# Input projection of a hybrid decoder layer: convolution passes alternate with value, gate and output gate passes

## The chip, the cores and the metric

The kernel runs on one core of one Trainium2 chip. The metric is the device time of one launch in microseconds. Five engines work side by side, each through its own queue in order: TensorE (PE, matmuls and transposes), VectorE (DVE), ScalarE (ACT), GpSimd (POOL) and SyncE (SP, which issues most of the DMAs). An instruction waits for its inputs by semaphores, and everything behind it on its engine waits with it. On-chip tiles come from pools: a name (or a tag) has a number of buffers (`bufs`), and a new tile of that name waits until the oldest one is no longer used.

## The reference

One inference step of a layer with two kinds of heads that share one input projection `z = x @ w_in` (1024 to 3600 columns) over 2048 prompt tokens and 64 sampled tokens:

```python
fq, fk, fv = z[..., 0:512], z[..., 512:1024], z[..., 1024:1536]      # attention heads
flogf = log_sigmoid(z[..., 1536:1544] + b_fox_f)
qk_in = z[..., 1544:2568]                                             # memory heads
xpad = concatenate([conv_prev, qk_in], axis=1)
conv = conv_b + xpad[:, 0:S] * conv_w[0]
for j in range(1, CONV_WIDTH):
    conv = conv + xpad[:, j:j + S] * conv_w[j]
qk = silu(conv)
mv = z[..., 2568:3080]
ig, lf = z[..., 3080:3084] + b_ig, log_sigmoid(z[..., 3084:3088] + b_fg)
og = sigmoid(z[..., 3088:] + b_og)
```

Then come attention with forget gates over the prompt (`_fox_prompt`) and, for the sampled tokens, over 8192 cached positions in pages (`_fox_sample`); the matrix memory in chunks (`_mlstm_chunk`: gates, `Wqk @ v + q @ C`, normaliser, new `C` and `n`); the output projection with a layer norm; and an MLP with squared ReLU and a second layer norm. Keys, values, gates, memory states and the last three convolution inputs are outputs too.

## The kernel before

The kernel has four phases: A, the input projection; B, the prompt's attention (`phase_b`); O, the output projection (`phase_o`); C, the MLP (`phase_c`). The change lies in phase A, which takes up to 991 us.

**Blocks and passes.** `block_a(bi)` (L395) handles one of four blocks of 512 prompt tokens; block 0 has the 64 sampled tokens too (`pre`, tile 16). The block's input stands transposed in `xT[bi]`, split into a high and a low part. A pass takes 256 columns of `w_in`: `wload` (L212) loads them in two halves, ACT makes the high part (`whi`, L130), DVE the low one (`wlo`, L133), and `mm3` (L137) does three matmuls for each product (L138 to L140). Passes are of two layouts. In `natural` (L399) tokens are the output's partitions, and a `sink` takes each token tile out of PSUM; in the convolution and query loops columns are the partitions, with groups of 256 tokens (320 with the sampled ones). All results go through four PSUM buffers of one tag, `pm`. A block has 14 passes in this order:

- two value passes, v0 and v1 (L417 to L424); ACT copies the tiles out, SP stores them to `dv`; v1 carries 16 gate columns too, which DVE copies to `gat`;
- in block 0, `conv_setup` (L180) loads and transposes the convolution weights and old convolution inputs;
- four convolution passes, c0 to c3, of two column tiles `j` each (L429 to L464). ACT copies the sums to `qi` (L447); DVE does one multiplication with bias (L453), three multiply-adds over 128x512 (L455) and, after ACT's tanh (L457), the product (L458); SP stores `th` to `dqk` (L459). `ac` and `th` share the tag `ac` with three buffers. In block 0 there is a second, short convolution for the sampled tokens with each `j`, and then the new convolution state goes to `scT` (L464);
- the transposes of the convolution state for the outputs (L466 to L482), in blocks 0 and 3;
- `yield 1` (L483), by which `block_a` hands control back once;
- two output gate passes, og0 and og1 (L484 to L493): DVE adds the bias (L489), ACT does tanh (L490), DVE scales (L491), SP stores to `dog`; then `gated.add(bi)`;
- two query passes, two key passes and two value passes of the attention heads (L496 to L534); ACT takes the sums out, SP stores them.

**What runs beside the passes.** After each PSUM group a pass calls `tick(us)` (L109) with its nominal time: 2.6 for a token tile, 2.56 or 3.2 for a column group. Two streams of small work are generators that `tick` advances by a step. The memory stream `macc` makes a step per `PACE_M` = 2.3 us of ticks and holds a list: `gate_stream` (gates and their cumulated sums, put at the head of the list after v1, L427), then `m_block` of the block (L597), in block 0 preceded by the `prologue` of the sampled attention, and after block 0 `m_sample` (L677), which loads `state_C` into `C0` (L739) for each of four heads. `m_block` has 4 steps and then 7 for each chunk of 128 tokens: exponentials of the loaded `Wm` and `qa`, scores (L622), `while bi not in gated: yield 1` (L628), the load of the gates `og`, transposed keys (L635), outputs (L647, L648), normalising (`h_out`, `norm_out`, with POOL's product at L557), the new state (L656, L659); the transposes of the outputs (L562) are left to the next chunk (`turn_out`). The sampled attention `acc` makes a step per 7.5 us of ticks from the end of block 0 on: POOL gathers pages of keys (`kraw`, L1359), DVE transposes them (L1361), TensorE multiplies (L1372), and after eight pairs of pages there is a softmax (L1383: scores L1390, exponentials L1406, transposes L1416, L1433) and products with the values (L1451).

**What sets the order.** The program is recorded in this order, and a scheduler then places each engine's instructions by its own estimate of when their inputs are ready; `beside` (L102) keeps a stream's step behind the latest matmul, ACT split and DVE split of the pass. On the chip the order is fixed. The loop that drives it is at L807: `next(g)` runs a block up to its `yield 1`, then `m_block(bi)` is appended to the list, and `for _ in g` runs the rest.

```python
    for bi in range(4):
        g = block_a(bi)
        next(g)
        if bi == 0 and gen:
            macc[1].append(prologue(gen))
        macc[1].append(m_block(bi))
        for _ in g:
            pass
```

Of the kernel before, what the change touches and what calls it, by code (L numbers as in the profile page):

```python
# [23 lines left out]
PACE_M = 2.3  # L24
# [28 lines left out]
def body(ctx, tc, I, O, stages):  # L53
# [43 lines left out]

    acc = [0.0, None, PACE_A]
    macc = [0.0, []]
    last = {}  # L100

    def beside(gen):  # L102
# [6 lines left out]
    def tick(us):  # L109

        macc[0] += us
        while macc[1] and macc[0] > PACE_M:
            macc[0] -= PACE_M
            if beside(macc[1][0]) == 0:
                macc[1].pop(0)
        if not macc[1]:
            macc[0] = 0.0
        acc[0] += us
        while acc[1] is not None and acc[0] > acc[2]:
            acc[0] -= acc[2]  # L120
            if beside(acc[1]) == 0:
                acc[1] = None
# [14 lines left out]
    def mm3(ps, wh, wl, xh, xl, first, stop):  # L137
        T.matmul(ps, wh, xh, start=first, stop=False)  # L138
        T.matmul(ps, wh, xl, start=False, stop=False)  # L139
        last["PE"] = T.matmul(ps, wl, xh, start=False, stop=stop)  # L140
# [254 lines left out]
    def block_a(bi):  # L395
# [18 lines left out]
            A.copy(st, ps)  # L414
            return st

        for i in range(2):  # L417
            def sink(t, m, ps, i=i):
                r = tok_r(t)
                SY.dma_start(dv[r:r + m, i * 256:(i + 1) * 256], stage(ps[:, :256], m, 256))  # L420
                if i == 1:
                    V.tensor_copy((gats if t == 16 else gat[:, t])[:, 0:16], ps[:, 256:272])
            natural(sink, (C_V + i * 256, 256), *([(C_FF, 8), (C_I, 8)] if i == 1 else []),
                    hook=None if i else lambda n: load_x(bi, blk[n + 2:n + 3]))  # L424
        if bi == 0:
            conv_setup()
        macc[1].insert(0, gate_stream(bi))  # L427

        for j in range(8):  # L429
            if j % 2 == 0:  # L430
                wh, wl = wload([(C_QK + j * 128, 256)])
            cs = slice((j % 2) * 128, (j % 2) * 128 + 128)
            qi = pa.tile([128, 515], F32, name="qi", bufs=2)
            V.tensor_copy(qi[:, 0:3], hist[:, j])
            if pre:
                qs = pa.tile([128, 8, 11], F32, name="qs", bufs=2)
                V.tensor_copy(qs[:, :, 0:3], scT[:, j])
            for i in range(2):
                xh, xl = xT[bi][i]
                w = 256 + (pre if i == 0 else 0)  # L440
                ps = ppa.tile([128, 512], F32, name="pm", tag="pm", bufs=4)[:, :w]
                for k in range(8):
                    mm3(ps, wh[k][:, cs], wl[k][:, cs], xh[:, k, :w], xl[:, k, :w], k == 0, k == 7)
                tick(w * 0.01)
                if w == 320:
                    A.copy(qs[:, :, 3:11], ps[:, 0:64].rearrange("p (b t) -> p b t", t=8))
                A.copy(qi[:, 3 + i * 256:259 + i * 256], ps[:, w - 256:])  # L447
            V.tensor_copy(hist[:, j], qi[:, 512:515])

            def conv(src, dst, n):  # L450
                ac = pa.tile([128, 512], F32, name="ac", tag="ac", bufs=3)[:, :n]
                acv = ac if len(src(0).shape) == 2 else ac.rearrange("p (b t) -> p b t", t=8)
                V.tensor_scalar(acv, src(0), cw[:, j, 0:1], cw[:, j, 4:5], op0=OP.mult, op1=OP.add)  # L453
                for q in range(1, 4):
                    V.scalar_tensor_tensor(acv, src(q), cw[:, j, q:q + 1], acv, op0=OP.mult, op1=OP.add)  # L455
                th = pa.tile([128, 512], F32, name="th", tag="ac", bufs=3)[:, :n]
                A.activation(th, ac, AF.Tanh)  # L457
                V.scalar_tensor_tensor(th, th, 1.0, ac, op0=OP.add, op1=OP.mult)  # L458
                SY.dma_start(dst, th)  # L459

            conv(lambda q: qi[:, q:q + 512], dqk[j, :, t0:t0 + 512], 512)
            if pre:
                conv(lambda q: qs[:, :, q:q + 8], dqk[j, :, S:], 64)
                V.tensor_copy(scT[:, j], qs[:, :, 8:11])  # L464

        if pre:  # L466

            cs_n = pa.tile([24, 1024], F32, name="cs_n", tag="xn", bufs=2)
            for hf in range(2):
                pc = ppa.tile([24, 512], F32, name="px", tag="pm", bufs=4)  # L470
                for j in range(4):
                    T.transpose(pc[:, j * 128:(j + 1) * 128], scT[:, hf * 4 + j].rearrange("p b k -> p (b k)"), ident)
                A.copy(cs_n[:, hf * 512:(hf + 1) * 512], pc)
            SY.dma_start(O["conv_sample"].rearrange("l b j c -> (l b j) c"), cs_n)
        if bi == 3:
            ch_n = pa.tile([3, 1024], F32, name="ch_n", tag="xn", bufs=2)
            for hf in range(2):
                pc = ppa.tile([3, 512], F32, name="px", tag="pm", bufs=4)
                for j in range(4):
                    T.transpose(pc[:, j * 128:(j + 1) * 128], hist[:, hf * 4 + j], ident)  # L480
                A.copy(ch_n[:, hf * 512:(hf + 1) * 512], pc)
            SY.dma_start(O["conv_prompt"].rearrange("l b j c -> (l b j) c"), ch_n)  # L482
        yield 1  # L483
        for i in range(2):  # L484
            def sink(t, m, ps, i=i):
                r = tok_r(t)
                cs = slice(i * 256, (i + 1) * 256)
                st = pa.tile([128, 256], F32, name="st", bufs=4)[:m]
                V.tensor_tensor(st, ps, bog[:m, cs], op=OP.add)  # L489
                A.activation(st, st, AF.Tanh, scale=0.5)  # L490
                V.scalar_tensor_tensor(st, st, 1.0, nwh[:m, cs], op0=OP.add, op1=OP.mult)  # L491
                SY.dma_start(dog[r:r + m, cs], st)
            natural(sink, (C_O + i * 256, 256))  # L493
        gated.add(bi)

        for j in range(4):  # L496
            if j % 2 == 0:
                wh, wl = wload([(j * 128, 256)])
                if pre:
                    qr = ps_.tile([32, 8, 8, 8], F32, name="qr", bufs=1)  # L500
            cs = slice((j % 2) * 128, (j % 2) * 128 + 128)
            st = pa.tile([128, 512], F32, name="qst", tag="ac", bufs=3)
            for i in range(2):
                xh, xl = xT[bi][i]
                w = 256 + (pre if i == 0 else 0)
                ps = ppa.tile([128, 512], F32, name="pm", tag="pm", bufs=4)[:, :w]
                for k in range(8):
                    mm3(ps, wh[k][:, cs], wl[k][:, cs], xh[:, k, :w], xl[:, k, :w], k == 0, k == 7)
                tick(w * 0.01)
                if w == 320:  # L510
                    for c in range(4):
                        V.tensor_scalar(qr[:, :, (j % 2) * 4 + c], ps[c * 32:c * 32 + 32, 0:64].rearrange("p (b t) -> p b t", t=8), 0.125, None, op0=OP.mult)
                A.activation(st[:, i * 256:i * 256 + 256], ps[:, w - 256:], AF.Copy, scale=0.125)
            SY.dma_start(dq[j, :, t0:t0 + 512], st)
            if pre and j % 2 == 1:
                SY.dma_start(dqb[0, :, :, j // 2 * 64:j // 2 * 64 + 64].rearrange("b p c -> p b c"), qr.rearrange("p b i t -> p b (i t)"))
        for i in range(2):
            def sink(t, m, ps, i=i):
                d = k_out(t)[:, i * 256:(i + 1) * 256]
                if t == 16:  # L520
                    if i == 0:
                        sqk.append(ps_.tile([64, 512], F32, name="sqk", tag="vt", bufs=2))
                    st = sqk[0][:, i * 256:(i + 1) * 256]
                    A.copy(st, ps)
                else:
                    st = stage(ps, m, 256)
                SY.dma_start(d, st)
            natural(sink, (512 + i * 256, 256))
        for i in range(2):
            def sink(t, m, ps, i=i):  # L530
                d = v_out(t)[:, i * 256:(i + 1) * 256]
                SY.dma_start(d, stage(ps, m, 256))
            natural(sink, (1024 + i * 256, 256),
                    hook=None if i == 0 or bi == 3 else lambda n: load_x(bi + 1, BLKS[bi + 1][0:1]) if n == len(blk) - 1 else None)  # L534

    dgs_s = drm.tile([4, 8], F32, name="dgs_s")

# [267 lines left out]
    first = [wload([(C_V, 256)])]  # L805
    load_x(0, [0])
    for bi in range(4):  # L807
        g = block_a(bi)
        next(g)
        if bi == 0 and gen:  # L810
# [701 lines left out]
```

## Time and profile before

| | |
|---|---|
| median of 3 runs | 3477.34 us (3472.2 to 3483.77) |
| profiled execution | 3490.14 us, its span 3488.4 us |
| mean granted TensorE clock | 0.98 |
| phase A | from 13.4 us (first projection matmul) to 991.2 us (last one) |
| HBM traffic | 598.01 MB read, 61.22 MB written, 189 GB/s over the span |

In the profile an engine is busy while it executes an instruction; waiting, branching and issuing of DMAs do not count. A window's row gives the length, the busy time of PE, PEld (weight loads, which overlap PE), DVE, ACT and POOL with the number of instructions, the clock granted to TensorE (1.00 is full), the busy share of the DMA engines and GB/s. A row of waits has the engine and the line that waited, what released it, the sum in us, how often, and the longest. A row of the chain or of the timeline has the start, the duration and the work. `pm<-whi,xh` is a tile and what it is made from.

### The profile page before, as it was taken

To read this page: it belongs to the slowest core of one execution; us is meant where nothing else is said; L and a number is where in the kernel's file an instruction comes from. 1 tells how busy PE (TensorE), PEld (TensorE's weight loads), DVE (VectorE), ACT (ScalarE), POOL (GpSimd) and SP (SyncE) were. 2 spreads that over 40 slices of the span, in tenths; PEclk is the share of its full clock that TensorE was granted. 3 is DMA by queue.
4 is the path that set the end of the run, shared out by engine and by line. 5 is a ranking of instruction groups with operands and counts; after the bars stand their busy time and mean duration, and the time that the engine had idled before them with its cause. 6 is when DMAs were issued, how large, how long until landed. Compare 5 with 4: busy or idle time off the path is not lost.

```text
span 3488.4 us, 59559 instructions
## 1 busy us (share of the span) xinstructions
PE 3347.1 (96%) x22428; PEld 2674.8 (77%) x22428; DVE 2176.1 (62%) x5282; ACT 1369.4 (39%) x2818; POOL 903.2 (26%) x962
## 2 busy tenths in 40 slices
PE   8899899999989999999899999999999999999998
PEld 8898788888876666667567677776677777788887
DVE  5847756657568787655556567656666544654555
ACT  3332233334358888512323233332233333343332
POOL 0023222321332222266332324313334111100000
PEclk9999899999999999999899999999999999999999
DMA  5567786775853232586776767858768555442221
GB/s 175 167 172 231 224 248 222 240 227 189 277 165 86 76 81 58 169 289 228 264 237 200 266 215 263 281 181 281 241 218 300 183 174 174 140 154 73 85 85 64
DMA packets 446040, 663.15 MB, mean 190 GB/s; under 512 B 84604, under 2 KB 333760, under 8 KB 444856
## 3 DMA queue, kind: packets, MB, share of 16 engines
q1 hardware_dynamic: 369064, 380.13, 36.2%
q0 software_dynamic: 74304, 270.57, 22.3%
q10 hardware_dynamic: 2384, 8.65, 0.7%
q8 instruction: 176, 2.88, 0.3%
q14 instruction: 112, 0.92, 0.1%
HBM read 598.01 MB, written 61.22 MB: 189 GB/s over the span
## 4 chain that ended last, share of the span: by engine, by line
PE 66%; DMA 13%; issue 5%; DVE 4%; POOL 2%; ACT 1%; SPq 0%; POOLq 0%; ACTq 0%; another core or an unknown queue 0%; DVEq 0%
PE py L138 6%; PE py L140 6%; PE py L139 6%; DMA kraw<-cache_k,idxK 6%; PE ph L138 5%; PE ph L139 5%; PE ph L140 5%; PE po L960 4%; PE pt L951 4%; PE sO L1451 3%; PE pm L138 3%; PE pm L140 3%; PE pm L139 3%; DMA vt<-cache_v,idxV 3%; PE sQ L1372 2%
## 5 line engine op out<-in xcount | busy, mean ns | idle before, releaser
L1191 DVE TENSOR_TENSOR y<-y,py 128x512 f32<-128x512 f32 (+1 forms) x476 | 319.5, 680 | 257.2 <-PE py L140 253.0
L130 ACT ACTIVATE wh<-wr 128x1024 fp32r<-128x1024 f32 x264 | 273.6, 1056 | 481.1 <-PE py L140 261.0
L138 PE MATMUL ph<-x1h,wh 128*128 128x512 f32 (+1 forms) x1280 | 456.9, 357 | 3.4 <-ACT wh L130 3.4
L139 PE MATMUL ph<-x1l,wh 128*128 128x512 f32 (+1 forms) x1280 | 456.1, 356 | 0.0
L140 PE MATMUL ph<-x1h,wl 128*128 128x512 f32 (+1 forms) x1280 | 454.4, 356 | 0.2 <-DVE wl L133 0.2
L1446 POOL DMA_INDIRECT vt<-cache_v,idxV x256 | 264.4, 1033 | 701.0 <-PE sO L1451 665.2
L1361 DVE STREAM_TRANSPOSE kT<-kraw 128x512 f32<-128x512 f32 x512 | 327.6, 684 | 179.7 <-DMA kraw<-cache_k,idxK 178.8
L138 PE MATMUL py<-wh,hh 128*128 128x512 f32 (+1 forms) x1088 | 431.1, 398 | 2.8 <-DVE y L1189 1.6
L1359 POOL DMA_INDIRECT kraw<-cache_k,idxK x256 | 281.4, 1099 | 576.9 <-DVE kT L1361 431.8
L139 PE MATMUL py<-wl,hh 128*128 128x512 f32 (+1 forms) x1088 | 428.9, 394 | 0.7 <-DVE wl L133 0.7
L140 PE MATMUL py<-wh,hl 128*128 128x512 f32 (+1 forms) x1088 | 428.9, 394 | 0.0
L133 DVE TENSOR_TENSOR wl<-wr,wh 128x1024 fp32r<-128x1024 f32 x264 | 333.4, 1269 | 97.2 <-PE ph L140 33.2
L138 PE MATMUL pm<-whi,xh 128*128 128x256 f32 (+2 forms) x1088 | 322.9, 297 | 4.8 <-ACT qi L447 2.2
L140 PE MATMUL pm<-whi,xl 128*128 128x256 f32 (+2 forms) x1088 | 314.4, 289 | 0.0
L139 PE MATMUL pm<-wlo,xh 128*128 128x256 f32 (+2 forms) x1088 | 314.2, 289 | 0.0
L138 PEld LDWEIGHTS ph<-x1h,wh 128*128 128x128 f32 x1280 | 241.6, 189 | 48.0 <-issue 11.9
L140 PEld LDWEIGHTS ph<-x1h,wl 128*128 128x128 f32 x1280 | 241.4, 189 | 42.7 <-issue 11.1
L139 PEld LDWEIGHTS ph<-x1l,wh 128*128 128x128 f32 x1280 | 241.7, 189 | 40.7 <-issue 8.6
L138 PEld LDWEIGHTS py<-wh,hh 128*128 128x128 f32 (+1 forms) x1088 | 200.9, 185 | 64.4 <-issue 18.5
L140 PEld LDWEIGHTS py<-wh,hl 128*128 128x128 f32 (+1 forms) x1088 | 200.9, 185 | 55.5 <-issue 9.9
L139 PEld LDWEIGHTS py<-wl,hh 128*128 128x128 f32 (+1 forms) x1088 | 201.1, 185 | 48.4 <-issue 8.6
L138 PE MATMUL pm<-xh,whi 128*128 128x256 f32 (+1 forms) x768 | 226.9, 295 | 0.0
(358 smaller groups left out, 6864.3 us busy)
## 6 DMA issues: line engine op xcount, KB each, us to landing
wr<-w SPq DMA_DIRECT2D x256, 512.0 KB
wra<-w_in SPq DMA_DIRECT2D x112, 512.0 KB
xn<-x_prompt SPq DMA_DIRECT2D x32, 512.0 KB
Rb<-dR SPq DMA_DIRECT2D x128, 128.0 KB
dqk<-th SPq DMA_DIRECT2D x32, 256.0 KB
qk<-dqk SPq DMA_DIRECT2D x16, 512.0 KB
qn<-dq SPq DMA_DIRECT2D x128, 64.0 KB
wr<-w_o SPq DMA_DIRECT2D x16, 512.0 KB
```

Of the source, the lines that this page charges most:

```text
L130: last["ACT"] = A.activation(dst, src, AF.Copy, scale=scale)
L133: r = (eng or V).tensor_tensor(dst, src, hi.bitcast(F32), op=OP.subtract)
L138: T.matmul(ps, wh, xh, start=first, stop=False)
L139: T.matmul(ps, wh, xl, start=False, stop=False)
L140: last["PE"] = T.matmul(ps, wl, xh, start=False, stop=stop)
L951: T.transpose(pt[:, k], sc[i][0][k0 // 4][:, k * 128:(k + 1) * 128], ident)
L960: last["PE"] = T.matmul(po[c:c + 64, q0:], z["vn"][:, k], PT[:, k - k0, q0:], start=(k < 2), stop=(k >= nk - 2), skip_group_check=True)
L1191: V.tensor_tensor(y, y, ps, op=OP.add)
L1359: G.indirect_dma_start(out=kraw, out_offset=None, in_=ck, in_offset=IO(ap=idxK[:, b, kt + k, f:f + 1], axis=0))
L1361: V.transpose(z["kT"][:, k, 2 * f + i].rearrange("p b c -> p (b c)"), kraw[:, i * 512:(i + 1) * 512])
L1446: G.indirect_dma_start(out=vt.rearrange("p f c -> p (f c)"), out_offset=None, in_=cv, in_offset=IO(ap=idxV[:, b, pg * 4 + u, f:f + 1], axi ...
L1451: T.matmul(po[r:r + 32], z["PT"][:, hg, 2 * f + g, pg].rearrange("p h q -> p (h q)"), vt[:, g, hg * 256:(hg + 1) * 256], start=(kt == 0 an ...
```

## The change

Each kind of pass becomes a function (`v_pass`, `conv_pass`, `conv_end`, `og_pass`, `q_pass`, `fk_pass`, `fv_pass`) with the body it had; `conv_pass(jj)` does the two column tiles 2 jj and 2 jj + 1. The passes are then called in another order: v0, c0, v1, c1, og0, c2, og1, c3 in place of v0, v1, c0, c1, c2, c3, og0, og1. `conv_setup` runs after v0, the gate stream still enters after v1, `gated` is set after og1. `yield 1` comes after the last convolution pass and `conv_end`, so `m_block` (and in block 0 the prologue) enters the list only after the output gates. In block 3 the memory stream's pace is 0.8 times 2.3 us. Queries, keys and values of the attention heads keep their order.

```diff
+    mpace = [PACE_M]
@@
-        while macc[1] and macc[0] > PACE_M:
-            macc[0] -= PACE_M
+        while macc[1] and macc[0] > mpace[0]:
+            macc[0] -= mpace[0]
@@
-        for i in range(2):
-            def sink(t, m, ps, i=i):
+        def v_pass(i):
+            def sink(t, m, ps):
...
-        if bi == 0:
-            conv_setup()
-        macc[1].insert(0, gate_stream(bi))
-
-        for j in range(8):
-            if j % 2 == 0:
-                wh, wl = wload([(C_QK + j * 128, 256)])
+        def conv_pass(jj):
+            for j in (2 * jj, 2 * jj + 1):
+                if j % 2 == 0:
+                    wh, wl = wload([(C_QK + j * 128, 256)])
...
-        yield 1
-        for i in range(2):
-            def sink(t, m, ps, i=i):
+        def og_pass(i):
+            def sink(t, m, ps):
...
-        gated.add(bi)
+            if i == 1:
+                gated.add(bi)
...
+        v_pass(0)
+        if bi == 0:
+            conv_setup()
+        conv_pass(0)
+        v_pass(1)
+        macc[1].insert(0, gate_stream(bi))
+        conv_pass(1)
+        og_pass(0)
+        conv_pass(2)
+        og_pass(1)
+        conv_pass(3)
+        conv_end()
+        yield 1
+        for i in range(2):
+            q_pass(i)
+        for i in range(2):
+            fk_pass(i)
+        for i in range(2):
+            fv_pass(i)
@@
     for bi in range(4):
+        if bi == 3:
+            mpace[0] = 0.8 * PACE_M
         g = block_a(bi)
         next(g)
```

More of the change, by code (lines that the diff above doesn't have):

```diff
@@ L424, in block_a @@
                     hook=None if i else lambda n: load_x(bi, blk[n + 2:n + 3]))
-        if bi == 0:
-            conv_setup()
-        macc[1].insert(0, gate_stream(bi))
-        for j in range(8):
-            if j % 2 == 0:
-                wh, wl = wload([(C_QK + j * 128, 256)])
-            cs = slice((j % 2) * 128, (j % 2) * 128 + 128)
-            qi = pa.tile([128, 515], F32, name="qi", bufs=2)
-            V.tensor_copy(qi[:, 0:3], hist[:, j])
-            if pre:
-                qs = pa.tile([128, 8, 11], F32, name="qs", bufs=2)
-                V.tensor_copy(qs[:, :, 0:3], scT[:, j])
-            for i in range(2):
[L439 to L482, printed above, removed]
-        yield 1
-        for i in range(2):
-            def sink(t, m, ps, i=i):
+        def conv_pass(jj):
+            for j in (2 * jj, 2 * jj + 1):
+                if j % 2 == 0:
+                    wh, wl = wload([(C_QK + j * 128, 256)])
+                cs = slice((j % 2) * 128, (j % 2) * 128 + 128)
+                qi = pa.tile([128, 515], F32, name="qi", bufs=2)
+                V.tensor_copy(qi[:, 0:3], hist[:, j])
+                if pre:
+                    qs = pa.tile([128, 8, 11], F32, name="qs", bufs=2)
+                    V.tensor_copy(qs[:, :, 0:3], scT[:, j])
+                for i in range(2):
+                    xh, xl = xT[bi][i]
+                    w = 256 + (pre if i == 0 else 0)
+                    ps = ppa.tile([128, 512], F32, name="pm", tag="pm", bufs=4)[:, :w]
+                    for k in range(8):
+                        mm3(ps, wh[k][:, cs], wl[k][:, cs], xh[:, k, :w], xl[:, k, :w], k == 0, k == 7)
+                    tick(w * 0.01)
+                    if w == 320:
+                        A.copy(qs[:, :, 3:11], ps[:, 0:64].rearrange("p (b t) -> p b t", t=8))
+                    A.copy(qi[:, 3 + i * 256:259 + i * 256], ps[:, w - 256:])
+                V.tensor_copy(hist[:, j], qi[:, 512:515])
+                def conv(src, dst, n):
+                    ac = pa.tile([128, 512], F32, name="ac", tag="ac", bufs=3)[:, :n]
+                    acv = ac if len(src(0).shape) == 2 else ac.rearrange("p (b t) -> p b t", t=8)
+                    V.tensor_scalar(acv, src(0), cw[:, j, 0:1], cw[:, j, 4:5], op0=OP.mult, op1=OP.add)
+                    for q in range(1, 4):
+                        V.scalar_tensor_tensor(acv, src(q), cw[:, j, q:q + 1], acv, op0=OP.mult, op1=OP.add)
+                    th = pa.tile([128, 512], F32, name="th", tag="ac", bufs=3)[:, :n]
+                    A.activation(th, ac, AF.Tanh)
+                    V.scalar_tensor_tensor(th, th, 1.0, ac, op0=OP.add, op1=OP.mult)
+                    SY.dma_start(dst, th)
+                conv(lambda q: qi[:, q:q + 512], dqk[j, :, t0:t0 + 512], 512)
+                if pre:
+                    conv(lambda q: qs[:, :, q:q + 8], dqk[j, :, S:], 64)
+                    V.tensor_copy(scT[:, j], qs[:, :, 8:11])
@@ new lines, in conv_end @@
+        def conv_end():
+            if pre:
+                cs_n = pa.tile([24, 1024], F32, name="cs_n", tag="xn", bufs=2)
+                for hf in range(2):
+                    pc = ppa.tile([24, 512], F32, name="px", tag="pm", bufs=4)
+                    for j in range(4):
+                        T.transpose(pc[:, j * 128:(j + 1) * 128], scT[:, hf * 4 + j].rearrange("p b k -> p (b k)"), ident)
+                    A.copy(cs_n[:, hf * 512:(hf + 1) * 512], pc)
+                SY.dma_start(O["conv_sample"].rearrange("l b j c -> (l b j) c"), cs_n)
+            if bi == 3:
+                ch_n = pa.tile([3, 1024], F32, name="ch_n", tag="xn", bufs=2)
+                for hf in range(2):
+                    pc = ppa.tile([3, 512], F32, name="px", tag="pm", bufs=4)
+                    for j in range(4):
+                        T.transpose(pc[:, j * 128:(j + 1) * 128], hist[:, hf * 4 + j], ident)
+                    A.copy(ch_n[:, hf * 512:(hf + 1) * 512], pc)
+                SY.dma_start(O["conv_prompt"].rearrange("l b j c -> (l b j) c"), ch_n)
@@ L493, in block_a @@
             natural(sink, (C_O + i * 256, 256))
-        gated.add(bi)
[L496 to L516, printed above, removed]
@@ L517, in block_a, with q_pass @@
-        for i in range(2):
-            def sink(t, m, ps, i=i):
+            if i == 1:
+                gated.add(bi)
+        def q_pass(jj):
+            for j in (2 * jj, 2 * jj + 1):
+                if j % 2 == 0:
+                    wh, wl = wload([(j * 128, 256)])
+                    if pre:
+                        qr = ps_.tile([32, 8, 8, 8], F32, name="qr", bufs=1)
+                cs = slice((j % 2) * 128, (j % 2) * 128 + 128)
+                st = pa.tile([128, 512], F32, name="qst", tag="ac", bufs=3)
+                for i in range(2):
+                    xh, xl = xT[bi][i]
+                    w = 256 + (pre if i == 0 else 0)
+                    ps = ppa.tile([128, 512], F32, name="pm", tag="pm", bufs=4)[:, :w]
+                    for k in range(8):
+                        mm3(ps, wh[k][:, cs], wl[k][:, cs], xh[:, k, :w], xl[:, k, :w], k == 0, k == 7)
+                    tick(w * 0.01)
+                    if w == 320:
+                        for c in range(4):
+                            V.tensor_scalar(qr[:, :, (j % 2) * 4 + c], ps[c * 32:c * 32 + 32, 0:64].rearrange("p (b t) -> p b t", t=8), 0.125, None, op0=OP.mult)
+                    A.activation(st[:, i * 256:i * 256 + 256], ps[:, w - 256:], AF.Copy, scale=0.125)
+                SY.dma_start(dq[j, :, t0:t0 + 512], st)
+                if pre and j % 2 == 1:
+                    SY.dma_start(dqb[0, :, :, j // 2 * 64:j // 2 * 64 + 64].rearrange("b p c -> p b c"), qr.rearrange("p b i t -> p b (i t)"))
@@ L519, in sink, with fk_pass @@
+        def fk_pass(i):
+            def sink(t, m, ps):
                 d = k_out(t)[:, i * 256:(i + 1) * 256]
@@ L528, in block_a, with fv_pass, sink @@
             natural(sink, (512 + i * 256, 256))
-        for i in range(2):
-            def sink(t, m, ps, i=i):
+        def fv_pass(i):
+            def sink(t, m, ps):
                 d = v_out(t)[:, i * 256:(i + 1) * 256]
@@ L534, in block_a @@
                     hook=None if i == 0 or bi == 3 else lambda n: load_x(bi + 1, BLKS[bi + 1][0:1]) if n == len(blk) - 1 else None)
+        v_pass(0)
[13 more added lines that the diff above has]
+            q_pass(i)
+        for i in range(2):
+            fk_pass(i)
+        for i in range(2):
+            fv_pass(i)
     dgs_s = drm.tile([4, 8], F32, name="dgs_s")
@@ L807, in body @@
     for bi in range(4):
+        if bi == 3:
+            mpace[0] = 0.8 * PACE_M
         g = block_a(bi)
```

## The prediction

> **What bounds the kernel now.** I read the page first, then TensorE's time stretch by stretch, then who it waits for, then the chain around one long gap.
>
> ```profile
> span 3488.4 us, 59559 instructions
> PE 3347.1 (96%) x22428; PEld 2674.8 (77%) x22428; DVE 2176.1 (62%) x5282; ACT 1369.4 (39%) x2818; POOL 903.2 (26%) x962
> ```
>
> TensorE (PE) is the bound, and its matmuls are not changed here. What the order of passes can move is its idle time and its granted clock. The input projection runs from 13.4 to 991.2 us. I cut it at the passes' borders: rows 2, 4, 6, 8 run, for blocks 0 to 3, from the first convolution pass through the output gates to the end of the first query pass; the other rows hold the second query pass, the keys and values of the attention heads and the value passes of the next block.
>
> ```profile
> core 0: us, PE busy (x) PEld busy (x) DVE busy (x) ACT busy (x) POOL busy (x), PEclk, DMA share, GB/s
> 13.40:49.30 35.90, 34.18 (x275) 33.77 (x273) 11.18 (x18) 12.37 (x22) 4.44 (x4) 1.00 0.73 225
> 49.30:166.60 117.30, 103.87 (x770) 101.03 (x770) 99.66 (x325) 37.06 (x82) 5.89 (x6) 0.93 0.50 144
> 166.60:293.50 126.90, 120.85 (x1015) 118.06 (x1013) 65.38 (x186) 45.20 (x102) 29.90 (x44) 0.99 0.66 192
> 293.50:431.70 138.20, 121.03 (x1025) 107.81 (x1023) 107.93 (x288) 36.12 (x72) 35.65 (x34) 0.92 0.73 227
> 431.70:557.10 125.40, 122.18 (x1009) 108.91 (x1008) 62.37 (x177) 45.28 (x107) 33.32 (x42) 0.98 0.80 241
> 557.10:679.90 122.80, 114.61 (x975) 104.20 (x972) 90.82 (x241) 40.88 (x87) 38.09 (x33) 0.96 0.71 224
> 679.90:794.60 114.70, 111.08 (x984) 103.41 (x983) 58.51 (x156) 40.00 (x86) 34.18 (x40) 1.00 0.79 243
> 794.60:909.60 115.00, 106.89 (x962) 95.92 (x960) 80.98 (x193) 44.40 (x95) 26.56 (x28) 0.96 0.66 211
> 909.60:991.20 81.60, 79.93 (x694) 74.58 (x691) 37.60 (x127) 25.10 (x63) 26.88 (x30) 1.00 0.74 220
> ```
>
> Length minus PE busy is 13.4, 17.2, 8.2 and 8.1 us in the four convolution stretches, 46.9 us together, against 16.2 us in all the others. There the clock also falls to 0.92 to 0.96; busy time times (1 - clock) is 7.3 + 9.7 + 4.6 + 4.3 = 25.9 us. So 72.8 us are lost in 493.3 us of convolution stretches (15%), and about 20 us in the other 484.5 (4%). VectorE (DVE) is busy 0.70 to 0.85 of the former and about 0.5 of the latter. Inside a stretch it is worse; these are a value pass, a convolution pass and an output gate pass of block 3:
>
> ```profile
> 781.60:794.60 13.00, 13.00 (x109) 12.43 (x106) 3.60 (x8) 3.10 (x5) 2.83 (x4) 1.00 0.90 298
> 807.70:821.70 14.00, 14.00 (x121) 12.80 (x120) 13.89 (x37) 4.02 (x7) 1.20 (x1) 1.00 0.47 144
> 874.50:892.00 17.50, 17.50 (x168) 14.61 (x167) 11.73 (x27) 4.16 (x7) 7.54 (x8) 1.00 1.00 326
> ```
>
> DVE needs 13.89 us of a 14.00 us convolution pass, and four such passes follow each other: what it falls behind, it cannot make up until they end. Who TensorE waits for during the projection:
>
> ```profile
> PE sT L1416 <- ACT Sn L1406: 8.1, 1, 8.1
> PE px L472 <- ACT qi L447: 7.6, 1, 7.6
> PE mm L746 <- DMA C<-state_C: 7.3, 2, 5.4
> PE mm L562 <- POOL hh L557: 6.5, 4, 2.4
> PE mn L656 <- ACT hh L579: 6.0, 2, 5.5
> PE mr L316 <- DVE rows L323: 4.3, 1, 4.3
> PE mm L622 <- DMA qk<-dqk: 1.2, 1, 1.2
> DVE ac L453 <- DMA dqk<-th: 22.8, 8, 8.4
> ```
>
> The last row is DVE's own wait: the ring of three `ac`/`th` tiles. Each convolution takes two of them, so it starts in the buffer whose store to `dqk` was issued two convolutions before. The chain around the gap at 604 us shows what that does:
>
> ```profile
> 588.89 0.61 DVE th L458
> 589.67 13.20 DMA dqk<-th
> 602.89 0.55 DVE ac L453
> 603.51 0.59 DVE th L458
> 604.29 1.23 PE mn L656 x4
> ```
>
> One late store (13.20 us) stops DVE; the memory stream's `dn` and `hh` stand behind it, and PE at L656 behind those.
>
> **The change, part by part.** It adds and removes no matmul, copy or load: each block keeps its 14 passes, so TensorE's work is unchanged, and I cost the reordering itself at 0.
>
> *Alternating passes* attacks the gaps. These windows hold one or two long gaps each, and the clock they cost:
>
> ```profile
> 82.00:92.00 10.00, 5.73 (x32) 5.46 (x32) 6.45 (x21) 0.89 (x2) 0.00 (x0) 0.83 0.41 127
> 109.00:127.00 18.00, 8.84 (x47) 7.45 (x46) 16.00 (x45) 4.72 (x11) 2.27 (x2) 0.62 0.52 165
> 339.00:352.00 13.00, 9.86 (x57) 9.39 (x56) 10.59 (x27) 3.49 (x6) 5.47 (x4) 0.74 0.77 236
> 365.00:372.00 7.00, 5.70 (x34) 4.66 (x36) 6.28 (x15) 2.12 (x4) 2.83 (x2) 0.76 0.49 154
> 377.00:389.00 12.00, 9.08 (x62) 8.82 (x62) 6.21 (x14) 2.22 (x6) 4.42 (x4) 0.86 0.71 213
> 418.00:434.00 16.00, 10.59 (x83) 9.85 (x83) 5.45 (x19) 6.57 (x20) 3.60 (x8) 0.68 0.76 250
> 598.00:608.00 10.00, 4.51 (x26) 4.31 (x25) 5.11 (x18) 1.80 (x6) 0.00 (x0) 0.83 0.84 279
> 636.00:645.00 9.00, 6.80 (x35) 6.59 (x35) 6.59 (x25) 3.39 (x10) 1.16 (x2) 0.62 0.73 266
> 840.00:854.00 14.00, 5.89 (x36) 5.62 (x35) 9.98 (x20) 7.72 (x22) 4.46 (x7) 0.63 0.68 198
> ```
>
> Idle plus busy times (1 - clock): 5.2, 12.5, 5.7, 2.7, 4.2, 8.8, 6.3, 4.8, 10.3 us, 60.5 us in sum. The fifth and sixth are mostly the loads of `state_C` (L746), which are as long after the change: 13.0 us stay. 47.5 us can go.
> - 598 us, 6.3 us: goes whole. With an og or v pass (over 13 us) between convolution passes, the store two convolutions back belongs to the pass before, in blocks 1 to 3; the longest store shown is 13.20 us, and the three passes above last 13.0, 14.0 and 17.5 us.
> - The other six, 41.2 us: DVE, or ACT behind DVE, is late. At best all goes. At worst nothing: DVE's work is the same, and block 0, with two convolutions per tile, still reuses a buffer within a pass. I take two thirds, 27.5 us. It is nearer to all because a convolution pass (13.89 us of DVE) and a value pass (3.60) or an output gate pass (11.73) now share 27 to 32 us of TensorE: 0.65 to 0.81 of DVE per pair, where it was 0.99 for single passes in a row. In block 3's softmax (840 us), the built order puts a whole output gate pass more between the scores (L1390) and the transposes (L1416).
>
> The clock's part is this trace's: the windows at 339 and 636 us have clock 0.74 and 0.62. By the Trainium skill ("TensorE: Matmul & The Clock Gate", "HAM oscillation — how this bites in real kernels"), the clock halves only behind TensorE gaps over about 3.4 us; the idle of these two is 3.1 and 2.2 us in all, so the trace disagrees. By that rule their clock loss of 5.1 us would have another cause and stay, and the sum would be 3 us smaller (two thirds of it).
>
> *The memory stream starts later.* `yield 1` now comes after all output gates, so `m_block` (32 steps, one per 2.3 us of ticks) enters at the query passes. Its three idle steps of waiting for `gated` go, but it loses the 20.8 us of ticks of the two og passes: blocks 0 to 2 push about five steps into the next block. Each chunk's loads (`va`, `Wm`, `qa`, `qk`, `og`) move with it on SP's queue, past the gate stores and among the query and key stores. Nothing waits for them but the stream itself, and TensorE where the stream's matmuls stand in its queue: L562 and L622, 7.7 us now. *Block 3 runs the stream at 0.8 of the pace* (1.84), so its 32 steps fit into 62.1 us of ticks, 33.7 steps, and the projection ends with the same tail. Bounds for both: 0 if the chains keep up, and a doubling, +7.7 us. I take +6: the steps are denser just where the cover of the og passes is gone.
>
> *`conv_end`* stays behind the fourth convolution pass, now before the queries, so the first query pass's matmuls stand behind its transposes in TensorE's queue, where a part of the transposes used to stand among the gates'; its 7.6 us wait is within the 12.5 us above, and is the part of it least sure to go. *`conv_setup`* comes a pass earlier. Its loads:
>
> ```profile
> 20.79 0.29 SPq L182 DMA_DIRECT2D cwn<-conv_w  x1
> 24.55 0.62 SPq L189 DMA_DIRECT2D scn<-state_conv  x1
> ```
>
> They are issued by 25 us, and the first value pass ends at 33 us: cost 0. If a load took 13.20 us like the slow store, 5 us.
>
> Sum: -6.3 - 27.5 + 6 = -27.8 us, so -28. The profiled execution, 3490.14 us (span 3488.4), would become 3462; it lies 0.37% over the median of 3477.34. The same -28 on the median gives **3449 us**.
>
> **Rivals.**
> *All of it goes* (0.20): the convolution stretches fall to the loss of the quiet ones, 4% of 493.3 = 20 us instead of 72.8, and no new cost: -53, **3424**. For it: in c1 of block 3, with DVE at 0.99, TensorE does not wait at all, so only a build-up over several passes costs. Against it: `state_C`'s 13.0 us stay, and the value passes lose their quiet.
>
> *Nothing net* (0.17): loss grows in a straight line with DVE's share. The stretch from v0 to og1 keeps the same DVE work, the waits only move into v and og passes, and the ring was the only real gain: -6.3 + 6, **3477**. Against it: between 781 and 822 us the passes with shares 0.28 and 0.99 both ran without idle time.
>
> *Slower* (0.17): the memory stream becomes the wait. From 909.6 us on, 51.8 us of ticks took 81.6 us, 1.58 us per tick; a chunk of seven steps at 1.84 then has 20.3 us, where at 2.3 it has 25.4. If a chunk's chain (loads, exponentials, POOL's product, norm, turn) takes longer than 20.3 us, each of the 16 chunks stops PE at L562 or L656 by the longest such row, 2.4 us: 38.4 - 13.7 us that the L562, L656 and L622 rows have now = +25, with nothing gained: **3502**. For it: four L562 waits exist already. Against it: only block 3 has the closer pace.
>
> **How the numbers follow.** Forecast 0.46 (gain of 10 to 45 us), then 0.20, 0.17, 0.17. 0.3% is 10.4 us, about what a measurement of this kernel can tell from no change: faster 0.66, same 0.17, slower 0.17. The range takes in the larger gain with the last third of the gaps (47.5 + 13.0 = 60.5, so 3417) and the first half of the slower case: 3415 to 3490.
>
> **What would show it.** The DVE wait on `dqk` falls from 22.8 us to under 8, all of it in block 0. In the stretches up to the last convolution pass, clock is 0.97 or more and idle under 25 us. The waits at the rows of L656, L316 and L1416 shrink to under 6 us together; `state_C`'s stays. The projection ends near 963 us instead of 991, and everything after it keeps its length. Wrong it would be if L562, L656 and L622 together exceed 20 us, or if DVE passes 0.9 in the alternating stretches.

## The result, and the profile after

The changed kernel takes 3484.15 us (median of 20 runs, 3475.89 to 3498.09) against 3476.62 us before (20 runs). The ratio is 1.0023 with a 95% interval of 1.0014 to 1.0033: 5 to 11 us slower. The forecast was 28 us faster.

The profiled execution has a span of 3477.5 us. Its projection runs from 13.2 to 994.3 us, 981.1 us in place of 977.8: the gain did not come. To see where it went I cut both projections at the same places: from each block's first value pass to the end of its first query pass (v0 to q0, which holds all the passes whose order changed), and from the second query pass to the block's end (q1 to fv1, whose passes kept theirs). Windows of before, blocks 0 to 3, with the columns of the prediction's tables:

```profile
core 0: us, PE busy (x) PEld busy (x) DVE busy (x) ACT busy (x) POOL busy (x), PEclk, DMA share, GB/s
13.40:166.60 153.20, 138.05 (x1043) 134.80 (x1042) 110.84 (x343) 49.43 (x103) 10.32 (x10) 0.94 0.56 163
166.60:262.30 95.70, 89.68 (x750) 88.67 (x748) 47.00 (x140) 35.97 (x85) 19.48 (x24) 1.00 0.63 176
262.30:431.70 169.40, 152.19 (x1286) 137.19 (x1287) 126.31 (x333) 45.35 (x89) 46.06 (x55) 0.92 0.74 230
431.70:523.00 91.30, 88.08 (x729) 76.60 (x728) 43.98 (x127) 31.01 (x72) 21.49 (x28) 0.99 0.82 242
523.00:679.90 156.90, 148.71 (x1253) 136.51 (x1252) 109.21 (x291) 55.15 (x122) 49.93 (x48) 0.96 0.72 227
679.90:765.70 85.80, 82.18 (x728) 77.22 (x726) 46.94 (x130) 32.31 (x73) 27.57 (x33) 1.00 0.82 246
765.70:909.60 143.90, 135.79 (x1219) 122.11 (x1216) 92.55 (x219) 52.08 (x109) 33.17 (x35) 0.96 0.67 216
909.60:991.20 81.60, 79.93 (x694) 74.58 (x691) 37.60 (x127) 25.10 (x63) 26.88 (x30) 1.00 0.74 220
```

The same cut of the changed kernel:

```profile
13.20:158.80 145.60, 133.04 (x1032) 130.84 (x1030) 104.60 (x311) 51.05 (x103) 9.12 (x9) 0.98 0.55 162
158.80:247.40 88.60, 86.29 (x705) 85.68 (x705) 42.52 (x125) 29.03 (x64) 12.03 (x14) 0.98 0.64 183
247.40:409.90 162.50, 143.27 (x1298) 130.33 (x1296) 129.11 (x348) 48.32 (x96) 50.73 (x57) 0.97 0.75 232
409.90:508.50 98.60, 94.14 (x733) 79.42 (x733) 46.00 (x134) 30.53 (x75) 23.02 (x30) 0.96 0.77 240
508.50:664.60 156.10, 148.11 (x1259) 135.46 (x1258) 111.71 (x299) 56.12 (x127) 47.85 (x52) 0.97 0.72 227
664.60:756.80 92.20, 84.36 (x719) 77.25 (x717) 44.16 (x116) 30.72 (x68) 24.55 (x26) 0.98 0.80 250
756.80:891.30 134.50, 133.28 (x1175) 121.69 (x1173) 95.37 (x236) 52.91 (x114) 37.34 (x39) 0.99 0.65 205
891.30:994.30 103.00, 93.43 (x784) 84.27 (x783) 43.91 (x146) 27.79 (x69) 29.82 (x34) 0.95 0.67 210
```

The odd rows (v0 to q0) sum to 623.4 us before and 598.7 after: 24.7 us gained, and most of it is clock, which was 0.92 to 0.96 and is 0.97 to 0.99 (0.95 to 0.99 in the two repeats below); idle, length minus PE busy, went only from 48.7 to 41.0 us. The even rows (q1 to fv1) sum to 354.4 and 382.4 us: 28.0 us lost in passes whose order is the same. There idle rose from 14.5 to 24.2 us and the clock fell in every block, to 0.95 to 0.98. Block 3 alone went from 81.6 to 103.0 us. TensorE's largest waits in the changed kernel's projection:

```profile
PE px L263 <- DMA xn<-x_prompt: 8.9, 3, 4.7
PE mm L773 <- DMA C<-state_C: 8.6, 2, 7.3
PE pm L139 <- ACT qst L518: 6.8, 3, 5.1
PE mm L589 <- POOL hh L584: 6.6, 4, 4.3
PE mn L683 <- ACT hh L606: 6.4, 3, 3.2
PE mm L649 <- DMA qk<-dqk: 4.8, 1, 4.8
PE mg L387 <- DVE rows L355: 3.6, 1, 3.6
PE sQ L1401 <- DVE dn L603: 3.3, 1, 3.3
PE sQ L1401 <- DVE kT L1390: 3.3, 3, 2.3
PE mm L589 <- DVE Cs L686: 3.2, 1, 3.2
PE sT L1316 <- DVE tt L1315: 2.2, 2, 2.0
PE mr L317 <- DVE rows L324: 1.5, 2, 0.8
```

(L589, L649, L662, L683 are before's L562, L622, L635, L656.) The 8.1 us in front of block 3's softmax are gone and the 7.6 us at the convolution state's transposes too, though 6.8 us in front of query matmuls (released by `qst`) are new, 5.1 of them in block 0. `qst` shares the ring of the tag `ac` with the convolution's tiles, and the queries now follow the last convolution pass directly; how much of these 6.8 us is due to that, no run separates. The memory stream's rows, L589 twice, L683 and L649, now sum to 21.0 us where they had 13.7. DVE's own wait for the stores to `dqk` fell from 22.8 us:

```profile
DVE ac L454 <- DMA dqk<-th: 3.5, 2, 2.1
```

The two long gaps of block 3's last stretch, from the chain of waits, with POOL's row of the second:

```profile
894.20 15.61 DMA qk<-dqk
909.85 0.98 PE mm L649 x4
...
923.46 11.38 DMA Wm<-dM
934.92 1.29 ACT Wm L641 x4
936.33 0.62 POOL Wm L642
938.32 1.24 POOL hh L584
939.61 1.12 PE mm L589 x4
936.32 0.63 POOL L642 TENSOR_SCALAR_AFFINE_SELECT Wm<-Wm 128x512 f32<-128x512 f32 x1 [6.83 <-ACT Wm L641]
```

The first is the load of the block's first `qk`, issued once the last convolution's store is on its way (888.4 us); it takes 15.61 us, TensorE reaches L649 first and waits 4.8 us. In the kernel before, the same load is issued at 873.1 us, lands within 4.1 us, and TensorE is in the gate passes until 892 us. In the second gap, `Wm` of the second chunk takes 11.38 us to load. The mask of `Wm` (L642) stands ahead of `hh` of the first chunk (L584) in POOL's order; POOL idles 6.83 us until `Wm` has come and then does `hh`, so a load for the next chunk delays the normalising of this one, and TensorE waits at L589 for `hh`.

### The profile page after: what moved, and what is told of

Same layout as the page of the kernel before. It is cut to its first block, busy times and chain, and to the rows that moved or that the text cites. A ratio compares the mean times of both kernels' runs of the same rounds, so it can differ in the third digit from the quotient of the medians.

```text
span 3477.5 us, 59545 instructions
## 1 busy us (share of the span) xinstructions
PE 3343.5 (96%) x22428; PEld 2668.6 (77%) x22428; DVE 2178.8 (63%) x5282; ACT 1367.7 (39%) x2818; POOL 893.8 (26%) x962
## 4 chain that ended last, share of the span: by engine, by line
PE 74%; DMA 12%; DVE 6%; issue 4%; POOL 1%; ACT 1%; SPq 0%; POOLq 0%; ACTq 0%; DVEq 0%
PE py L139 7%; PE py L141 6%; PE py L140 6%; PE ph L139 6%; PE ph L140 6%; PE ph L141 6%; PE pm L139 4%; PE po L989 4%; PE pm L140 4%; PE pm L141 4%; PE pt L980 4%; DMA kraw<-cache_k,idxK 4%; PE sO L1480 4%; DMA vt<-cache_v,idxV 3%; PE sQ L1401 2%
## 5 line engine op out<-in xcount | busy, mean ns | idle before, releaser
L139 PEld LDWEIGHTS py<-wh,hh 128*128 128x128 f32 (+1 forms) x1088 | 201.0, 185 | 64.0 <-issue 17.3
```

## The experiments

The columns: v0 to q0 and q1 to fv1 as cut above, summed over the blocks (from unrounded times, so up to 0.1 us off the sums above); the time at which the first score matmul of the prompt's attention starts; the length of the output projection, with TensorE's wait of 2.3 to 2.4 us for its first weights; the span. Each is one profiled execution. The last column is the ratio of unprofiled runs to before's on the same chip.

| run | v0 to q0 | q1 to fv1 | attention starts | output projection | span | ratio (95%) |
|---|---|---|---|---|---|---|
| before, first profile | 623.5 | 354.3 | 999.9 | 224.6 | 3488.4 | 1 |
| before, second | 623.7 | 362.0 | 1007.1 | 223.1 | 3485.1 | |
| before, third | 624.3 | 353.4 | 998.4 | 225.0 | 3468.2 | |
| changed, first | 598.8 | 382.3 | 1002.5 | 223.6 | 3477.5 | 1.0023 (1.0014 to 1.0033) |
| changed, second | 601.8 | 384.5 | 1007.8 | 223.3 | 3480.4 | |
| changed, third | 601.1 | 378.6 | 1001.2 | 224.4 | 3482.3 | |
| e1 late stream alone | 610.1 | 373.9 | 1005.1 | 225.1 | 3479.9 | 1.0018 (1.0003 to 1.0034) |
| e2 pace alone | 620.2 | 353.6 | 995.0 | 234.1 | 3481.3 | 1.0033 (1.0020 to 1.0046) |
| e3 changed, full pace | 605.9 | 366.0 | 1005.8 | 226.1 | 3484.4 | 1.0056 (1.0038 to 1.0074) |
| e4 second gate pass last | 587.6 | 367.9 | 984.0 | 222.8 | 3451.1 | 0.9957 (0.9941 to 0.9973) |
| e5 block 3 as in e4 | 605.4 | 364.8 | 997.9 | 232.7 | 3485.5 | 1.0041 (1.0026 to 1.0057) |
| e6 run of three | 616.8 | 356.2 | 994.1 | 228.7 | 3486.5 | 1.0022 (1.0011 to 1.0033) |
| e7 e4 again | 594.7 | 362.5 | 984.7 | 224.1 | 3464.2 | |

**Repeats: r1 and r3 (before), r2 and r4 (changed).** No edit.

> The kernel before once more, for a second profile: its first profiled execution lay 14 us over its median. Theory 'its excess lay behind the projection': the projection takes 973 to 981 us again and what follows it 2472 to 2480 us instead of 2488. Rival 'its projection was slow': the projection takes 960 to 968 us, and what follows 2486 to 2490 us.

> The changed kernel once more. Theory 'loss moved from the alternating stretches to those from the second query pass on': v0 to q0 again 590 to 607 us in sum, q1 to fv1 again 374 to 390 us. Rival 'chance of one execution': q1 to fv1 under 365 us in sum.

> The kernel before a third time, same theories as for its second profile; v0 to q0 615 to 630 us in sum, q1 to fv1 348 to 358 us by both.

> The changed kernel a third time, same theories as for its second profile.

The shift from one stretch to the other repeats. Means of three: v0 to q0 623.8 before and 600.6 after (-23.2), q1 to fv1 356.6 and 381.8 (+25.2), start of the attention 1001.8 and 1003.8 (+2.0). Both block 3 waits come again in r2:

```profile
PE mm L589 <- POOL hh L584: 5.5, 2, 4.9
PE mm L649 <- DMA qk<-dqk: 4.4, 1, 4.4
```

What follows the start of the attention took 2488.5, 2478.0 and 2469.8 us before, so the first profile's excess over its median lay mostly behind the projection; that spread within one kernel is larger than the measured difference. The second profile's projection, 985.6 us, lay outside the ranges of both theories.

**e1, late stream alone.** The passes stand as before; the hand-back moves behind the gates, and the pace of block 3 is 0.8. The difference from the kernel before, without the lines that define `mpace` and use it in `tick`:

```diff
         if bi == 3:
             ch_n = ...
-        yield 1
         for i in range(2):
...
             natural(sink, (C_O + i * 256, 256))
         gated.add(bi)
+        yield 1
...
+        if bi == 3:
+            mpace[0] = 0.8 * PACE_M
```

> Passes in the order of before; only the memory stream is moved: m_block enters after the output gates, and block 3 runs at 0.8 of the pace. Theory 'the late stream eats the gain': the stretches from the second query pass to the last value pass lengthen by 20 to 30 us against before (354 us), the convolution stretches stay as lossy as before (clock 0.92 to 0.96), so the kernel is 15 to 35 us slower than before. Rival 'the late stream is free and the reordering itself gains nothing': within 7 us of before, and those stretches within 8 us of 354.

Neither theory has it whole. q1 to fv1 lengthens by 17.3 us against the mean of before (373.9 - 356.6), so the late stream is not free; but v0 to q0 shortens by 13.7 us (610.1 against 623.8), though four convolution passes still stand in a row and DVE still waits for their stores. Of these 13.7 us, 9.7 fall in block 0 (145.0 us against a mean of 154.7), whose row follows; DVE is busy 99.98 us in it where it was busy 110.84 (first row of the first table above).

```profile
DVE ac L454 <- DMA dqk<-th: 20.8, 8, 7.6
```

```profile
13.20:158.20 145.00, 135.52 (x1030) 132.72 (x1028) 99.98 (x298) 46.80 (x96) 7.77 (x7) 0.96 0.56 163
```

Moving the stream alone moves the loss: +3.3 us to the start of the attention. Against this one profile of e1, the reordering itself gives another 9.5 us in v0 to q0 (600.6) and takes 7.9 in q1 to fv1 (381.8); in block 3 that stretch is 89.1 us in e1 and 103.0 in the changed kernel. In e1 the two gate passes still stand between the last convolution and the stream, and the load of block 3's first `qk` is issued at 874.5 us, 37 us ahead of its scores; in the changed kernel it is 16 us.

**e2, pace alone.** The kernel before with the change's `mpace` lines (0.8 of the pace in block 3) and nothing else.

> The kernel before, with block 3's memory stream at 0.8 of the pace and nothing else. Theory 'the pace is what makes the late stream wait': block 3 from the second query pass on gets longer than 81.6 us by 5 to 15 us, or its convolution stretch does, and the kernel is 5 to 12 us slower. Rival 'only the late start counts': within 5 us of before.

Block 3 takes 225.4 us where it took 225.5, so the closer pace by itself costs nothing there, as long as the stream starts on time. The kernel is 0.33% slower all the same, and not in the projection: its attention starts 6.8 us earlier than before's mean, but its output projection takes 234.1 us in place of 223 to 225. Waits of TensorE in that phase, e2 and then before's third profile:

```profile
PE sO L1454 <- DMA vt<-cache_v,idxV: 8.6, 4, 2.9
```

```profile
PE sO L1451 <- DMA vt<-cache_v,idxV: 3.4, 5, 1.3
```

The scheduler has placed later instructions otherwise too, though no line of that phase was touched: from 1000 us to the end of that phase SyncE issues in the same order in the profiles of before, and in another order in e2. The wait for gathered values of the sampled attention explains 5.2 of the 9 us or so. e5 has the same (232.7 us).

**e3, the changed kernel at full pace.**

```diff
-        if bi == 3:
-            mpace[0] = 0.8 * PACE_M
```

> The changed kernel without the 0.8 pace in block 3. Theory 'the close pace makes TensorE wait': block 3 from the second query pass on falls from 103 us to 85 to 92 us, but some five steps of the stream are left over and run uncovered after the last pass, 10 to 20 us before the prompt's attention starts; in all 0 to 8 us slower than the changed kernel. Rival 'pace is harmless, block 3 loses by the late start alone': that stretch stays over 97 us, the tail comes on top, 10 to 20 us slower than the changed kernel.

Block 3 and what is left of the stream behind it, up to the attention, in e3 and in the changed kernel:

```profile
764.30:984.90 220.60, 215.59 (x1916) 197.01 (x1915) 134.29 (x357) 77.09 (x174) 65.37 (x68) 0.99 0.70 218
984.90:1005.80 20.90, 10.48 (x58) 8.90 (x56) 8.87 (x35) 6.75 (x18) 8.37 (x15) 0.76 0.64 165
```

```profile
756.80:994.30 237.50, 226.71 (x1956) 205.97 (x1955) 139.28 (x381) 80.70 (x183) 67.17 (x73) 0.97 0.66 207
994.30:1002.50 8.20, 2.03 (x14) 1.19 (x13) 2.89 (x9) 2.11 (x5) 2.16 (x6) 0.78 0.50 138
```

At full pace block 3's last stretch falls from 103.0 to 83.8 us, and the tail grows from 8.2 to 20.9 us, half idle. Block and tail are 241.5 against 245.7 us; before had 225.5 + 8.7 = 234.2. A stream that starts late is paid either within the block or behind it. At full pace the two waits of block 3's last stretch are gone (no row at L649, 3.5 us at L589), although the load of the second `Wm` takes 11.6 us there too; so the close pace exposes them. e1, with the same pace but the gates between the convolutions and the stream, has 2.9 us of such waits in that stretch. e3 is about 11 us slower than the changed kernel (1.0056 against 1.0023), more than the theory expected, and the projection does not show that part.

**e4 and e7, the second gate pass last.** The passes alternate, but the last gate pass is kept back until the stream has entered; full pace. The differences of e4 to e6 are from the changed kernel.

```diff
         conv_pass(2)
-        og_pass(1)
         conv_pass(3)
         conv_end()
         yield 1
+        og_pass(1)
...
-        if bi == 3:
-            mpace[0] = 0.8 * PACE_M
```

> Alternating as far as it lets the stream start a pass earlier: v0, c0, v1, c1, og0, c2, c3, then m_block enters, then og1; full pace in block 3. Theory 'late stream': most of the 25 us that the alternating stretches gained stay, and the stretches from the second query pass on lose under 10 us against before, so 8 to 25 us faster than before. Rival 'the reordering gains nothing in sum, losses only move': within 7 us of before.

> e4 a second time: by 'the stretches changed, not chance', v0 to q0 580 to 595 us and q1 to fv1 360 to 372 us in sum, and the prompt's attention starts at 980 to 990 us; by 'chance of one execution', over 995 us.

0.9957 (0.9941 to 0.9973), about 15 us faster than before: it beats both kernels. v0 to q0 is 588 and 595 us, less than in the changed kernel, and q1 to fv1 368 and 363 us, of which the first is a little more than expected; e7 lies in all its ranges. e3 differs from e4 by the place of the second gate pass alone: against it v0 to q0 is 11 to 18 us shorter and the tail behind block 3 falls from 20.9 to 14.3 us, while q1 to fv1 stays (366.0 us in e3). So what the kept-back gate pass gives lies in v0 to q0 and in the tail. Whether v0 to q0 gains by the earlier stream, or because the queries no longer follow the last convolution in their shared ring (5.6 us of waits for `qst` in block 0 of e3, 3.6 in e4), was not tried. Block 3's two stretches in e4:

```profile
746.70:885.60 138.90, 133.36 (x1195) 120.15 (x1193) 95.01 (x225) 52.26 (x109) 36.42 (x36) 0.99 0.66 211
885.60:969.70 84.10, 82.47 (x718) 75.90 (x715) 39.37 (x130) 25.09 (x63) 27.93 (x33) 1.00 0.74 233
```

**e5, the changed order in blocks 0 to 2, e4's in block 3, full pace.**

```diff
         conv_pass(2)
-        og_pass(1)
+        if bi < 3:
+            og_pass(1)
         conv_pass(3)
         conv_end()
         yield 1
+        if bi == 3:
+            og_pass(1)
```

> The changed kernel in blocks 0 to 2; block 3 alone in the order of e4 (v0, c0, v1, c1, og0, c2, c3, then m_block, then og1) and at full pace. Theory 'the cost sits in block 3, where the late stream has to end with the block': block 3 takes 221 to 228 us instead of 237.5, and the prompt's attention starts 10 to 18 us earlier than with the changed kernel (1003.8 us, mean of three); 0 to 10 us faster than before. Rival 'the late start costs in every block': block 2 loses as much as block 3 did, the attention starts within 5 us of 1003.8.

Block 3 and its tail:

```profile
761.70:983.60 221.90, 219.71 (x1944) 200.36 (x1943) 138.99 (x371) 80.34 (x181) 66.97 (x74) 0.99 0.70 221
983.60:997.90 14.30, 5.15 (x30) 4.18 (x28) 5.56 (x21) 3.99 (x10) 4.96 (x9) 0.72 0.70 178
```

Block 3 takes 221.9 us as the theory said, and the attention starts 5.9 us earlier than the changed kernel's mean, not 10 to 18: part of the gain is given back in the tail of 14.3 us. But e3, which has full pace and the changed order in block 3 too, had 220.6 us there already: the shorter block comes from the pace, and the kept-back gate pass shortens the tail, by 6.6 us. The whole is slower than before, 1.0041, with 8 us more in the output projection, as in e2. q1 to fv1 of blocks 1 and 2 keeps what it lost (98.4 and 93.6 us here, 91.3 and 85.7 before). So block 3 is where the late stream costs most, but not the only place.

**e6, a run of three.** c0 alone is taken out of the run; the stream starts as before; full pace.

```diff
         conv_pass(1)
-        og_pass(0)
         conv_pass(2)
-        og_pass(1)
         conv_pass(3)
         conv_end()
         yield 1
+        og_pass(0)
+        og_pass(1)
```

> v0, c0, v1, c1, c2, c3, then m_block, then og0, og1; full pace: the stream starts where it did before, and only one of the four convolution passes is taken out of the run. Theory 'a run of convolution passes makes DVE late': three in a row keep most of the loss, v0 to q0 600 to 618 us in sum (before 624, e4 588), q1 to fv1 350 to 362; 5 to 18 us faster than before. Rival 'only the start of the stream counts, not the run': as fast as e4, v0 to q0 under 595 us.

In the projection the theory holds: 616.8 and 356.2 us, the attention 7.7 us earlier than before, and a run of three still has DVE behind its stores, where e4 has little of it (e6, then e4):

```profile
DVE ac L454 <- DMA dqk<-th: 24.5, 6, 9.8
```

```profile
DVE ac L454 <- DMA dqk<-th: 5.5, 2, 5.0
```

The kernel as a whole is not faster: 1.0022. Its output projection is 4 us longer; the rest stands in no row that I could hold against before.

## Why the prediction was wrong

*What bounds it, and why the convolution stretches lose:* right for DVE's waits. The wait for the ring of `ac`/`th` tiles fell from 22.8 to 3.5 us, as forecast (under 8), and stays at 20.8 and 24.5 us in e1 and e6, which keep a run. But e1 gains in v0 to q0 with that wait in place, so the wait alone does not set what TensorE loses there. Up to the last convolution pass the clock is 0.97 or more, as forecast, in all blocks but block 1 (0.96, and 0.94 in both repeats).

*Gain of the alternating stretches, 33.8 us (6.3 + 27.5):* too large. Measured 23.2 us, and e1 shows that 13.7 us come with the stream's later start alone; the new order itself is worth 9.5 us on top. Two thirds of the six gaps was too much, and I had given the passes' order a part that comes with the stream. In block 0 DVE has less to do then; in the later blocks it has not (over all four, DVE is busy 440.9 us in e1 and 438.9 before), and what gives their part is open. Up to the last convolution pass idle is 29.3 us where I expected under 25, and 41.0 us to the end of the first query pass: the softmax's 8.1 us and the transposes' 7.6 us went, L656's 6.0 us stayed (6.4 at L683), and others came (6.8 us of query matmuls behind `qst`, 3.3 us of the sampled attention's scores behind `dn`).

*"The memory stream starts later ... I take +6":* this is the step that failed. Measured +25.2 us in q1 to fv1, -6.9, +4.4, +6.0 and +21.7 us in blocks 0 to 3 (means of three); with the passes in their old order the late start, with the closer pace in block 3, gave +17.3 (e1), the pace alone nothing (e2). I had taken as its upper bound a doubling of the stream's waits that the trace showed (7.7 us), and the term has three parts, not one. In the first pair of profiles the idle rises by 9.7 us (14.5 to 24.2). The clock behind it falls in every block: its cost, busy time times (1 - clock), sums to 0.9 us before and 11.9 after. I had counted the clock for the gaps that go and left it out for those that come. The other 7 us are busy time: the stretches hold 40 more matmul instructions (2901 to 2941), 45 fewer in block 0 and 90 more in block 3 (694 to 784). A stream that starts later leaves its last steps to the next block, and block 3 has none behind it. The idle time in block 3, 9.6 us, is nearly all in the two waits shown above. Before, the block's first loads had landed while TensorE did gates; in the changed order nothing is left between the last convolution, whose result the stream loads, and the queries. My sign of being wrong, L562, L656 and L622 over 20 us together, came true: 21.0 us at L589, L683 and L649. The sum of 25.2 us is three times the bound.

*Pace:* cost 0 by itself (e2, block 3). With the late start it is a choice between 19.2 us within block 3 and 12.7 us more tail (e3), no cure for either.

*The rivals:* the one that came nearest is "slower": the memory stream did become the wait. Its condition was met in part: the scores of block 3's chunks follow each other at 19.3, 24.6 and 23.5 us, against the 20.3 us of the closer pace. Its price was not reached as it said: not each of 16 chunks stopped TensorE, and about two thirds of what the stretches lost is clock and moved work. That its 25 us agree with the measured 25.2 is luck. And it had nothing gained, while 23 us were. The two nearly cancel, which is why the projection ends within 2 us of before.

*What stays open:* the projection explains about 2 of the 7.5 us between the medians. Where the others lie three profiles of each kernel do not show: their mean spans are the same (3480.6 and 3480.1 us), and behind the projection, before alone varies by 19 us. That the stream's loads, and not its matmuls among the passes, make block 3's late stretch wait is read from the chains and from e3, and was not tried by itself; why the load of `qk` takes 15.61 us there and 4.1 before is not known.

## What to carry to other kernels

When work is moved out of a stretch, price the stretch it moves into by what its loads take when they have no margin, and count TensorE's clock for the new gaps as for the old ones. A wait row of the old trace is no bound for a stream that loses its cover. Count also the steps that a later start pushes past the end, where no further block takes them. When breaking a run of passes that overloads one engine, try keeping a pass back behind the last of them, so that the work that depends on their end can start beside it: here e4, with the last two convolution passes side by side and one gate pass behind them, is faster than both kernels (0.9957), and the full alternation is slower.

## What the runs showed that I had not expected

In block 3 of the changed kernel one load of 256 KB of `Wm` took 11.38 us and one of `qk`, 512 KB, 15.61 us. Most of the stream's loads took 4 to 9 us in both kernels, and before had two of `qk` of 11.2 and 11.3 us; the prediction's longest was a store of 13.20 us, and I had not put such a time into the price of any load of the stream. A change of pace in one block's side stream (e2) left that block as it was and made an untouched phase 9 us longer, 5.2 us of it in waits for gathered values: a kernel's time can move by 0.3% in a place that no line of the diff points to.
